# Block ends of the input projection set apart, its pools given back early, and 24 gate projections in front of the scan

## The chip, the core and the metric

One core of one Trainium2 chip runs the kernel. The metric is the device time of one execution in microseconds (us). PE is the matmul engine (TensorE), DVE VectorE, ACT ScalarE, POOL GpSimd, SP the queue that issues every DMA of this kernel.

## What is computed

One layer of a hybrid diffusion block, D = 1024, 2048 latent tokens behind 256 context tokens (2304 in all), float32. The first half matters here:

```python
h  = modulate(rmsnorm(x, norm1_g), shift1, scale1)      # and hc for the context
q, k, v, rw, gl = jnp.split(h @ w_in, IN_SPLITS, axis=-1)   # 512 | 128 | 128 | 1696 | 2048 columns
ya = latent_window_attention(q, k, v, kc, vc, sink)     # banded, |i-j| <= 128, plus all context keys
# rw: centred short conv, then decay, rate, key, value for RWKV-7
r_l, v_l, hg_l, kk_l, dirs_l = rwkv_prepare(short_conv(rw, conv_w), ...)
# one scan per direction; each latent scan starts from the context's final state
yr = rwkv_output(y_lat[0] + y_lat[1], ...)
ga, gr = sigmoid(gl) halves;  x = x + gate1 * ((ga * (ya @ Wa) + gr * (yr @ Wr)) @ Wo)
x = x + gate2 * sq_relu_mlp(modulate(rmsnorm(x, norm2_g), shift2, scale2), w_mlp_up, w_mlp_down)
```

The `gl` columns are the merge gates: 2048 columns for the 2048 latent tokens.

## The kernel before

Every large matmul runs in float32r with operands split in a high and a low part, three passes per k-tile (`gemm`, L210: lines 213, 214 and 215; k runs over 8 tiles, so one unit, 128 output columns for one token block, is 24 matmuls). ACT makes the high part of a weight (`w_hi`, L206), POOL the low part (`w_lo`, L207), from a 512 KB load (`w_raw`).

**First stage, the in-projection.** The 2304 tokens go in three passes of two token blocks each:

```python
THIRDS = (((0, 256), (256, 512)), ((1280, 384), (768, 512)), ((1664, 384), (2048, 256)))
```

(first token, number of tokens). `norm_block` (L170) loads a block's rows, scales them by the root mean square, transposes them on PE (`tr`, L184), modulates (`hf`, DVE) and splits into `hh` (ACT) and `hl` (POOL, L191). `hh`/`hl` have one buffer for the first block of a pass (tag a) and one for the second (tag b), so a block of the next pass can be written only when the block that held its buffer has had its last projection. `project` (L236) loads one 128-column group of weights after the other and uses each for all blocks that it is given. There are 36 groups: 0 to 13 the RWKV input `u`, 14 k, 15 v, 16 to 19 q, 20 to 35 the gates. Pass 0 and 1 run groups 0 to 19 for both blocks, then the gates for the one block that lies at or beyond latent token 1024, in pass 1 (1280, 384) alone; pass 2 runs its gates for both blocks at its very end. The gates of latent tokens 0 to 1023 aren't made here: `norm_block` writes those tokens' normed rows to DRAM (`h_d`).

`prepare` (L326) makes the scan's inputs for one window of 256 tokens: short conv, decay, keys, on DVE, ACT and POOL, with small matmuls (`ss`, `snt`, `vt`, `nb`, `zz`, `bon`) between; its results go to DRAM (`ka_d`, `rho_d`, `bk_d`, `v_d`). Windows 0 and 1 follow pass 0's projections, 2 to 5 pass 1's, 8, 7, 6 stand between pass 2's groups 0 to 19 and its gates in the program.

**Second stage, the scan.** 36 steps of 64 tokens, in both directions, in nine windows of four steps. For a window, `gram` (L504) loads `kg` and `bkg` and multiplies them into `ga`; `inverse` (L517) turns them into a triangular inverse, a chain of 31 pairs of DVE operations on `tn` and `itmp` (L531, L533) behind four transposes into `au` (L525). `before` prepares a step, `chain` (L617) advances the state: `ch` matmuls, L621 the first. Beside the steps, `beside(w)` places attention (one block of 128 queries per call), pieces of a modulation vector, and the gates of latent tokens 0 to 1023 as `gate` (L845): 4 blocks of 256 tokens times 16 column groups = 64, six per call in calls 0 to 10, each with its own weight load and split (`gw_hi`, `gw_lo`) and 24 matmuls of 256 columns.

**What sets the order.** The program is written in the sequence above, and a scheduler then fixes the instructions of each engine in one static order, from the waits that it derives; an engine never passes an instruction that waits. A pool gives memory that a later pool reuses, and the later pool's tiles wait for the release of what lay there. Before, all pools of the first stage are closed together (L480), after the last preparation and the last projection in the program; the scan's tiles (`rp`) lie where `hh` and `hl` were.

## Time and profile before

| | us |
|---|---|
| median of 3 runs (4350.85 to 4358.86) | 4355.5 |
| the profiled execution | 4356.59 |
| its span, first to last instruction | 4354.8 |
| PE busy | 3996.6 |
| first stage | 0 to 995 |
| from its last projection to the first `ch` matmul | 995 to 1129 |
| scan with attention and gates | 1129 to 2510 |
| output projections and MLP | 2510 to 4354 |

A view by stretches gives, for each stretch, the width and each engine's busy time in it, then the granted TensorE clock (1.00 is 2.4 GHz, 0.50 is 1.2 GHz). A matmul's listed duration is longer than the distance to the next one's start, since matmuls are pipelined; the cost of one in a row of them is the distance of the starts. A view of waits gives, for an engine, what its instructions waited for, total, times and the longest. In a timeline the brackets hold the idle time before the instruction and what ended it.

### The profile page before, as it was taken

To read this page: it belongs to the slowest core of one execution; us is meant where nothing else is said; L and a number is where in the kernel's file an instruction comes from. 1 tells how busy PE (TensorE), PEld (TensorE's weight loads), DVE (VectorE), ACT (ScalarE), POOL (GpSimd) and SP (SyncE) were. 2 spreads that over 40 slices of the span, in tenths; PEclk is the share of its full clock that TensorE was granted. 3 is DMA by queue.
4 is the path that set the end of the run, shared out by engine and by line. 5 is a ranking of instruction groups with operands and counts; after the bars stand their busy time and mean duration, and the time that the engine had idled before them with its cause. 6 is when DMAs were issued, how large, how long until landed. Compare 5 with 4: busy or idle time off the path is not lost.

```text
span 4354.8 us, 68914 instructions
## 1 busy us (share of the span) xinstructions
PE 3996.6 (92%) x27020; PEld 3152.5 (72%) x27020; DVE 2330.7 (54%) x3905; ACT 1339.7 (31%) x2390; POOL 1580.1 (36%) x1276
## 2 busy tenths in 40 slices
PE   7989969894999999999999969998999999999999
PEld 5868858783766666666666646777888888888887
DVE  2264286687567747657756446444443436443434
ACT  3353444553333233332222223332222123212121
POOL 3353554552332222322111146523433234433332
PEclk8979979895999989999999968999999999999999
DMA  6555556666644544555443245452211113221111
GB/s 216 142 187 158 160 158 189 175 198 185 160 137 139 149 137 119 162 141 154 146 135 97 84 142 185 157 178 75 82 54 58 39 54 121 73 63 49 48 49 49
DMA packets 633081, 544.70 MB, mean 125 GB/s; under 512 B 120500, under 2 KB 560532, under 8 KB 631732
## 3 DMA queue, kind: packets, MB, share of 16 engines
q1 hardware_dynamic: 632756, 540.29, 41.8%
q8 instruction: 213, 3.49, 0.3%
q14 instruction: 112, 0.92, 0.1%
HBM read 399.96 MB, written 140.18 MB: 124 GB/s over the span
## 4 chain that ended last, share of the span: by engine, by line
PE 58%; DVE 10%; DMA 4%; issue 2%; POOL 2%; ACT 1%; SPq 1%; POOLq 0%; DVEq 0%; ACTq 0%
PE fd L1186 5%; PE fd L1187 5%; PE fd L1188 5%; PE fu L213 5%; PE fu L214 5%; PE fu L215 5%; PE ops L791 3%; PE gb L610 2%; DVE tn L533 2%; DVE itmp L531 1%; DVE st L542 1%; PE sT L781 1%; PE mm L1101 1%; PE mm L1103 1%; PE mm L1102 1%
## 5 line engine op out<-in xcount | busy, mean ns | idle before, releaser
L213 PE MATMUL acc<-hh,w_hi 128*128 128x384 f32 (+6 forms) x1304 | 457.8, 353 | 27.7 <-DVE st L225 9.8
L214 PE MATMUL acc<-hl,w_hi 128*128 128x384 f32 (+6 forms) x1304 | 458.4, 352 | 11.2 <-POOL hl L191 7.4
L215 PE MATMUL acc<-hh,w_lo 128*128 128x384 f32 (+6 forms) x1304 | 453.3, 349 | 10.9 <-POOL w_lo L207 9.7
L1192 DVE TENSOR_TENSOR acc<-fd,acc 128x512 f32<-128x512 f32 x480 | 322.3, 686 | 246.6 <-PE fd L1188 244.0
L1176 DVE TENSOR_TENSOR g_l<-rl,g_h 128x512 fp32r<-128x512 f32 x128 | 163.0, 1275 | 486.1 <-POOL rl L1175 486.1
L213 PE MATMUL fu<-h2h,up_h 128*128 128x512 f32 x1024 | 403.3, 394 | 5.8 <-ACT rl L1173 5.8
L214 PE MATMUL fu<-h2l,up_h 128*128 128x512 f32 x1024 | 402.6, 393 | 0.0
L1186 PE MATMUL fd<-dn_h,g_h 128*128 128x512 f32 x1024 | 399.4, 390 | 3.0 <-DVE acc L1190 3.0
L215 PE MATMUL fu<-h2h,up_l 128*128 128x512 f32 x1024 | 402.0, 393 | 0.0
L1187 PE MATMUL fd<-dn_l,g_h 128*128 128x512 f32 x1024 | 399.4, 390 | 0.0
L1188 PE MATMUL fd<-dn_h,g_l 128*128 128x512 f32 x1024 | 397.8, 390 | 0.0
L1175 POOL TENSOR_TENSOR rl<-rl 128x512 f32<-128x512 f32 x128 | 146.6, 1146 | 473.6 <-ACT g_h L1174 473.5
L832 POOL TENSOR_TENSOR gw_lo<-gw_raw,gw_hi 128x1024 fp32r<-128x1024 f32 x64 | 152.3, 2381 | 441.5 <-ACT gw_hi L831 359.8
L207 POOL TENSOR_TENSOR w_lo<-w_raw,w_hi 128x1024 fp32r<-128x1024 f32 (+1 forms) x92 | 224.2, 2439 | 226.0 <-ACT w_hi L206 208.0
L213 PEld LDWEIGHTS acc<-hh,w_hi 128*128 128x128 f32 (+2 forms) x1304 | 257.3, 198 | 51.3 <-DVE st L225 7.8
L214 PEld LDWEIGHTS acc<-hl,w_hi 128*128 128x128 f32 (+2 forms) x1304 | 258.1, 198 | 34.2 <-POOL hl L191 12.3
L215 PEld LDWEIGHTS acc<-hh,w_lo 128*128 128x128 f32 (+2 forms) x1304 | 256.4, 197 | 32.7 <-POOL w_lo L207 11.6
L1173 ACT ACTIVATE rl<-fu 128x512 f32<-128x512 f32 x128 | 76.3, 598 | 661.0 <-PE fu L215 652.0
L1130 POOL TENSOR_TENSOR dn_l<-raw,dn_h 128x1024 fp32r<-128x1024 f32 x64 | 155.6, 2450 | 275.0 <-ACT dn_h L1129 275.0
L793 POOL TENSOR_TENSOR ts<-ts,pT 128x512 f32<-128x512 f32 x124 | 159.1, 1287 | 263.9 <-ACT pT L788 261.9
L213 PEld LDWEIGHTS fu<-h2h,up_h 128*128 128x128 f32 x1024 | 193.0, 188 | 49.3 <-ACT rl L1173 6.1
L1186 PEld LDWEIGHTS fd<-dn_h,g_h 128*128 128x128 f32 x1024 | 192.6, 188 | 44.2 <-DVE acc L1190 3.4
(301 smaller groups left out, 9154.7 us busy)
## 6 DMA issues: line engine op xcount, KB each, us to landing
w_raw<-in_w_in SPq DMA_DIRECT2D x74, 512.0 KB
gw_raw<-in_w_in SPq DMA_DIRECT2D x64, 512.0 KB
raw<-in_w_mlp_up SPq DMA_DIRECT2D x64, 512.0 KB
raw<-in_w_mlp_down SPq DMA_DIRECT2D x64, 512.0 KB
bk_d<-bk SPq DMA_DIRECT2D x36, 512.0 KB
bkg<-bk_d SPq DMA_DIRECT2D x72, 256.0 KB
w<-v_d SPq DMA_DIRECT2D x144, 128.0 KB
ada_w<-in_w_ada SPq DMA_DIRECT2D x32, 512.0 KB
```

The source lines that it names most:

```text
L207: pool.tensor_tensor(out=lo[:, :, :m], in0=raw[:, :, :m], in1=hi[:, :, :m].bitcast(F32), op=ALU.subtract)
L213: pe.matmul(ps[:m, :n], wh[:, k, :m], hh[:, k, :], start=(k == 0), stop=False)
L214: pe.matmul(ps[:m, :n], wh[:, k, :m], hl[:, k, :], start=False, stop=False)
L215: pe.matmul(ps[:m, :n], wl[:, k, :m], hh[:, k, :], start=False, stop=(k == KC - 1))
L793: pool.tensor_tensor(out=ts[:, g], in0=ts[:, g], in1=pT[g], op=ALU.add)
L832: pool.tensor_tensor(out=lo, in0=raw, in1=hi.bitcast(F32), op=ALU.subtract)
L1130: eng.tensor_tensor(out=lo, in0=raw, in1=hi.bitcast(F32), op=ALU.subtract)
L1176: dve.tensor_tensor(out=glo[:, j], in0=rl, in1=gh[:, j].bitcast(F32), op=ALU.subtract)
L1186: pe.matmul(ps, lh, dn[j][0][:, cs], start=(j == 0), stop=False)
L1187: pe.matmul(ps, lh, dn[j][1][:, cs], start=False, stop=False)
L1188: pe.matmul(ps, ll, dn[j][0][:, cs], start=False, stop=(j == FG - 1))
L1192: dve.tensor_tensor(out=acc[:, cs], in0=ps, in1=acc[:, cs], op=ALU.add)
```

## The change

Three edits.

The in-projection. From pass 1 on, groups 0 to 3 run for one block, then for the other, then groups 4 to 13 for both; at the end of pass 0 and 1, groups 14 to 19 (and the gates, where the block has them) run for one block, whose successor is then normed, and after that for the other, whose successor is normed next. `FIRST` says which ends first: in pass 0 the block of tag a, in pass 1 that of tag b. Weights of a group that serves the blocks one after the other are loaded and split twice: 112 loads in all where there were 92. The context block has no q, but `project` loads and splits a group's weights ahead of the test that skips it, so four loads of pass 0 serve no matmul.

The pools. `prep` and `prp` keep a stack of their own; all others of the first stage are in `pg1`, closed before it. The second stage's `attn`, `gates` and three PSUM pools open between the two closings; `rp`, `chp` and `auxp` (scan) open behind `p1.close()` and now lie where the preparation's tiles were.

The gates. 24 of the 64 gate projections stand in the program ahead of the scan's loop; the other 40 go four per call in calls 0 to 9.

```diff
     prep = p1.enter_context(tc.tile_pool(name="prep", bufs=1, side="right"))
-    wpool = p1.enter_context(tc.tile_pool(name="w1", bufs=2, side="right"))
-    xpool = p1.enter_context(tc.tile_pool(name="xin", bufs=4, side="right"))
+    prp = p1.enter_context(tc.tile_pool(name="prp", bufs=3, space=PSUM, side="right"))
+    pg1 = ExitStack()
+    wpool = pg1.enter_context(tc.tile_pool(name="w1", bufs=2, side="right"))
+    xpool = pg1.enter_context(tc.tile_pool(name="xin", bufs=4, side="right"))
...
-    hs = norms(THIRDS[0])
+    FIRST = (0, 1)
+    HEAD = 4
+    hs = [norm(0, 0), norm(0, 1)]
     for i, wins in enumerate(ready):
-        project(THIRDS[i], hs, groups[:20])
-        late = [(b, h) for b, h in zip(THIRDS[i], hs) if b[0] >= CTX + GL8R]
-        if i + 1 < len(THIRDS):
-            project(*zip(*late), groups[20:]) if late else None
-        if i + 1 < len(THIRDS):
-            hs = norms(THIRDS[i + 1])
+        blks = THIRDS[i]
+        if i == 0:
+            project(blks, hs, groups[:14])
+        else:
+            f = FIRST[i - 1]
+            project(blks[f:f + 1], hs[f:f + 1], groups[:HEAD])
+            project(blks[1 - f:2 - f], hs[1 - f:2 - f], groups[:HEAD])
+            project(blks, hs, groups[HEAD:14])
+        if i + 1 < len(THIRDS):
+            nxt = [None, None]
+            for b in (FIRST[i], 1 - FIRST[i]):
+                late = groups[20:] if blks[b][0] >= CTX + GL8R else []
+                project(blks[b:b + 1], hs[b:b + 1], groups[14:20] + late)
+                nxt[b] = norm(i + 1, b)
+            hs = nxt
+        else:
+            project(blks, hs, groups[14:20])
...
-    p1.close()
+    pg1.close()
...
     p2 = ExitStack()
-    rp = p2.enter_context(tc.tile_pool(name="rp", bufs=2, reuse_waits="tile"))
+    pg = ExitStack()
     ap_ = p2.enter_context(tc.tile_pool(name="attn", bufs=1, reuse_waits="tile"))
-    chp = p2.enter_context(tc.tile_pool(name="chp", bufs=1, space=PSUM, reuse_waits="tile"))
-    auxp = p2.enter_context(tc.tile_pool(name="auxp", bufs=2, space=PSUM, reuse_waits="tile"))
+    gap = pg.enter_context(tc.tile_pool(name="gates", bufs=1, reuse_waits="tile"))
...
+    p1.close()
+    rp = p2.enter_context(tc.tile_pool(name="rp", bufs=2, reuse_waits="tile", side="right"))
+    chp = p2.enter_context(tc.tile_pool(name="chp", bufs=1, space=PSUM, reuse_waits="tile", side="right"))
+    auxp = p2.enter_context(tc.tile_pool(name="auxp", bufs=2, space=PSUM, reuse_waits="tile", side="right"))
...
+    EARLY = 24
+    for t0, g in gate_work[:EARLY]:
+        if g == 0:
+            hs = load_h(t0)
+        gate(t0, g, *hs)
...
-        for t0, g in gate_work[6 * w:6 * w + 6]:
+        for t0, g in gate_work[EARLY + 4 * w:EARLY + 4 * w + 4]:
```

How the instructions stand at three places, the kernel before first and the changed one second each time.

**Place 1, POOL at the end of pass 0**, behind the `w_lo` of k for the context block. `w_lo_1313` is v before; in the changed kernel 1313, 1320, 1327 and 1334 are the context's unused q weights and 1431 is k for block (256, 512). `hl_1280` is the low part of pass 1's first block, `sw` and `st` belong to the rotary embedding of q, `sn` to the preparation.

```order
L207 TENSOR_TENSOR w_lo_1313<-w_raw_1315,w_hi_1314 128x1024
L207 TENSOR_TENSOR w_lo_1383<-w_raw_1385,w_hi_1384 128x1024
L224 TENSOR_TENSOR sw_1304<-sw_1304,cs_1302 128x512
L226 TENSOR_TENSOR st_1301<-st_1301,sw_1304 128x512
L207 TENSOR_TENSOR w_lo_1427<-w_raw_1429,w_hi_1428 128x1024
L207 TENSOR_TENSOR w_lo_1471<-w_raw_1473,w_hi_1472 128x1024
L224 TENSOR_TENSOR sw_1418<-sw_1418,cs_1416 128x512
L191 TENSOR_TENSOR hl_1280_1560<-hf_1589,hh_1280_1559 128x384
L226 TENSOR_TENSOR st_1415<-st_1415,sw_1418 128x512
L207 TENSOR_TENSOR w_lo_1515<-w_raw_1517,w_hi_1516 128x1024
L224 TENSOR_TENSOR sw_1462<-sw_1462,cs_1460 128x512
L191 TENSOR_TENSOR hl_1280_1560<-hf_1597,hh_1280_1559 128x384
```

```order
L208 TENSOR_TENSOR w_lo_1313<-w_raw_1315,w_hi_1314 128x1024
L366 TENSOR_TENSOR sn_1888<-sn_1888,expo_78 128x16
L208 TENSOR_TENSOR w_lo_1320<-w_raw_1322,w_hi_1321 128x1024
L192 TENSOR_TENSOR hl_1280_1342<-hf_1371,hh_1280_1341 128x384
L192 TENSOR_TENSOR hl_1280_1342<-hf_1379,hh_1280_1341 128x384
L208 TENSOR_TENSOR w_lo_1327<-w_raw_1329,w_hi_1328 128x1024
L192 TENSOR_TENSOR hl_1280_1342<-hf_1387,hh_1280_1341 128x384
L192 TENSOR_TENSOR hl_1280_1342<-hf_1395,hh_1280_1341 128x384
L208 TENSOR_TENSOR w_lo_1334<-w_raw_1336,w_hi_1335 128x1024
L192 TENSOR_TENSOR hl_1280_1342<-hf_1403,hh_1280_1341 128x384
L192 TENSOR_TENSOR hl_1280_1342<-hf_1411,hh_1280_1341 128x384
L208 TENSOR_TENSOR w_lo_1431<-w_raw_1433,w_hi_1432 128x1024
```

Before, splits whose groups serve (256, 512) follow one another; now four unused splits, the six `hl` and the `sn` stand between the context's v and the next split that a matmul needs.

**Place 2, PE at the end of pass 1**, where the last projection of (1280, 384) ends. `acc_4369` is its last unit before; `acc_6207@2048` the third unit of pass 2's head groups in the changed kernel.

```order
L215 MATMUL acc_4369<-hh_1280_1559,w_lo_4363 128x384
L360 MATMUL ss_ps_4954<-c1_1763,ksq_4971 128x2 x2
L213 MATMUL acc_6035<-hh_1664_4397,w_hi_6030 128x384
L360 MATMUL ss_ps_4954<-c1_1763,ksq_4981 128x2 x2
L360 MATMUL ss_ps_4954<-c1_1763,ksq_4991 128x2 x2
L214 MATMUL acc_6035<-hl_1664_4398,w_hi_6030 128x384
L215 MATMUL acc_6035<-hh_1664_4397,w_lo_6029 128x384
L213 MATMUL acc_6035<-hh_1664_4397,w_hi_6030 128x384
L184 MATMUL tr_4455<-ident_76,x_4399 128x128
L184 MATMUL tr_4455<-ident_76,x_4407 128x128
L184 MATMUL tr_4455<-ident_76,x_4415 128x128
L214 MATMUL acc_6035<-hl_1664_4398,w_hi_6030 128x384
```

```order
L214 MATMUL acc_6207<-hh_2048_3700,w_hi_6202 128x256
L215 MATMUL acc_6207<-hl_2048_3701,w_hi_6202 128x256
L454 MATMUL bon_ps_5391<-ks_5282,c1_1803 128x256
L185 MATMUL tr_4633<-ident_76,x_4577 128x128
L185 MATMUL tr_4633<-ident_76,x_4585 128x128
L185 MATMUL tr_4633<-ident_76,x_4593 128x128
L185 MATMUL tr_4641<-ident_76,x_4577 128x128
L185 MATMUL tr_4641<-ident_76,x_4585 128x128
L185 MATMUL tr_4641<-ident_76,x_4593 128x128
L216 MATMUL acc_6207<-hh_2048_3700,w_lo_6201 128x256
L214 MATMUL acc_6207<-hh_2048_3700,w_hi_6202 128x256
L215 MATMUL acc_6207<-hl_2048_3701,w_hi_6202 128x256
```

Before, the transposes of (1664, 384) stand inside the first unit of pass 2, which needs them; now they stand inside units of block (2048, 256), normed earlier, and units of (1664, 384) come four units later.

**Place 3, DVE between the last preparation and the scan.** `au`, `itmp` and `tn` are the inverse of window 0; `mm`, `pack`, `atmp`, `qB`, `rr` belong to attention block 0; `ka`, `rho`, `bk`, `ks` to the last preparation.

```order
L437 TENSOR_TENSOR ks_8363<-ta_8377,x3_8162 128x256
L525 STREAM_TRANSPOSE au_9643<-ga_9530 32x1024 x4
L425 SCALAR_TENSOR_TENSOR ka_8369<-kk_8361,ep_8382 128x4x64
L427 TENSOR_TENSOR rho_8370<-x3_8162,ep_8382 128x4x64
L437 TENSOR_TENSOR ks_8368<-ta_8399,x3_8172 128x256
L425 SCALAR_TENSOR_TENSOR ka_8369<-kk_8366,ep_8404 128x4x64
L427 TENSOR_TENSOR rho_8370<-x3_8172,ep_8404 128x4x64
L430 TENSOR_TENSOR bk_8371<-bk_8371,cum_8380 128x4x64
L438 TENSOR_TENSOR bk_8371<-ks_8363,cum_8380 128x4x64
L428 SCALAR_TENSOR_TENSOR bk_8421<-ta_8427,kk_8361 128x4x64
L430 TENSOR_TENSOR bk_8371<-bk_8371,cum_8402 128x4x64
L531 TENSOR_TENSOR itmp_9650<-tn_9644,au_9643 128x31
```

```order
L774 TENSOR_REDUCE mm_11371<-sc1_11436 128x1
L774 TENSOR_REDUCE mm_11371<-sc0_11435 128x1
L775 TENSOR_TENSOR mm_11371<-mm_11371 128x8
L776 TENSOR_TENSOR pack_11369<-mm_11371,nsink_9632 128x8
L777 TENSOR_TENSOR mm_11371<-sinkb_9633,pack_11369 128x8
L782 TENSOR_TENSOR atmp_11450<-mt_11448,cc_83 72x512
L789 TENSOR_TENSOR qB0_9653<-atmp_11450,qB0_9653 8x512 x2
L787 TENSOR_TENSOR rr0_9655<-atmp_11450,rr0_9655 8x512
L543 STREAM_TRANSPOSE au_9774<-ga_9661 32x1024 x4
L549 TENSOR_TENSOR itmp_9781<-tn_9775,au_9774 128x31
L551 TENSOR_TENSOR tn_9775<-tn_9775,itmp_9781 128x31
```

Before, the inverse starts in the middle of the last preparation; now it stands behind all of it (its last row is ten rows ahead of this piece) and behind attention block 0's row maxima.

## Rows read from the trace of the kernel before

**Rows 1.** The page, busy time of each engine, its share and instructions.

```profile
PE 3996.6 (92%) x27020; PEld 3152.5 (72%) x27020; DVE 2330.7 (54%) x3905; ACT 1339.7 (31%) x2390; POOL 1580.1 (36%) x1276
```

**Rows 2.** By stretches: width, PE, PEld, DVE, ACT, POOL busy, clock, DMA share, GB/s.

```profile
195.00:330.00 135.00, 118.34 (x515) 94.08 (x514) 81.66 (x144) 70.59 (x140) 79.85 (x83) 0.82 0.59 185
...
520.00:680.00 160.00, 116.58 (x585) 104.47 (x584) 125.77 (x233) 71.83 (x161) 82.03 (x90) 0.82 0.59 171
...
995.00:1129.00 134.00, 66.53 (x640) 52.96 (x641) 93.84 (x188) 45.57 (x94) 43.29 (x52) 0.63 0.57 165
1129.00:2510.00 1381.00, 1298.02 (x14059) 911.76 (x14055) 883.62 (x1680) 402.90 (x723) 349.95 (x241) 0.97 0.48 136
2510.00:4354.00 1844.00, 1772.68 (x7712) 1437.16 (x7712) 816.99 (x1038) 443.63 (x650) 714.00 (x486) 0.97 0.28 87
```

**Rows 3.** PE's waits in 520 to 680: total us, times, longest.

```profile
PE tr L184 <- DVE x L178: 11.0, 1, 11.0
PE acc L213 <- ACT w_hi L206: 4.8, 2, 4.6
PE acc L215 <- POOL w_lo L207: 4.7, 3, 2.5
PE acc L214 <- POOL hl L191: 2.8, 4, 1.4
PE acc L213 <- ACT hh L190: 2.7, 2, 1.5
PE tr L184 <- DVE hf L186: 2.4, 1, 2.4
```

**Rows 4.** PE's waits in 320 to 530, the one for weights.

```profile
PE acc L215 <- POOL w_lo L207: 2.3, 1, 2.3
```

**Rows 5.** Weight and block splits: count, duration in ns (least/median/most), first and last start.

```profile
L206 ACT ACTIVATE w_hi<-w_raw x86: 616/1057/1077, 104.1 to 975.8; 128x1024 fp32r<-128x1024 f32 x80, 128x512 fp32r<-128x512 f32 x3, 128x768 fp32r<-128x768 f32 x3
L207 POOL TENSOR_TENSOR w_lo<-w_raw,w_hi x86: 1283/2404/4042, 105.5 to 977.5; 128x1024 fp32r<-128x1024 f32 x80, 128x512 fp32r<-128x512 f32 x3, 128x768 fp32r<-128x768 f32 x3
...
L191 POOL TENSOR_TENSOR hl<-hf,hh x32: 729/1009/3647, 205.4 to 646.0; 128x384 fp32r<-128x384 f32 x16, 128x512 fp32r<-128x512 f32 x8, 128x256 fp32r<-128x256 f32 x8
```

**Rows 6.** PE's timeline near 986: start, duration; 256 and 384 columns.

```profile
986.04 0.28 PE L214 MATMUL acc<-hl,w_hi 128*128 128x256 f32 x1
986.16 0.28 PE L215 MATMUL acc<-hh,w_lo 128*128 128x256 f32 x1
...
986.63 0.34 PE L213 MATMUL acc<-hh,w_hi 128*128 128x384 f32 x1
986.81 0.34 PE L214 MATMUL acc<-hl,w_hi 128*128 128x384 f32 x1
```

**Rows 7.** PE's waits in 995 to 1129, two of them.

```profile
PE sc L746 <- DVE qA L732: 19.8, 1, 19.8
...
PE g L514 <- DMA bkg<-bk_d: 12.9, 4, 8.5
```

**Rows 8.** Timelines of DVE and PE: five marks from the last preparation to the scan.

```profile
995.06 0.17 DVE L364 TENSOR_SCALAR sn<-ss_ps 128x16 f32<-128x16 f32 x1 [5.89 <-PE ss_ps L360]
...
1036.70 7.62 DVE L525 STREAM_TRANSPOSE au<-ga 32x1024 f32<-32x1024 f32 x4
...
1056.45 0.42 DVE L454 TENSOR_TENSOR bon<-bon_ps,x 128x256 f32<-128x256 f32 x1
...
1099.42 6.08 DVE L542 STREAM_TRANSPOSE st<-tn 32x1024 f32<-32x1024 f32 x3
...
1128.79 0.27 PE L621 MATMUL ch<-w,kr 128*64 128x64 f32 x1
```

**Rows 9.** Timelines of DVE and POOL near 1079: the inverse beside a weight split.

```profile
1079.02 0.42 DVE L531 TENSOR_TENSOR itmp<-tn,au 128x247 f32<-128x247 f32 x1
...
1079.69 2.53 DVE L533 TENSOR_TENSOR tn<-tn,itmp 128x247 f32<-128x247 f32 x1
...
1079.59 4.84 POOL L832 TENSOR_TENSOR gw_lo<-gw_raw,gw_hi 128x1024 fp32r<-128x1024 f32 x2 [0.88 <-DMA ada_w<-in_w_ada]
```

More of the change, by code (lines that the diff above doesn't have):

```diff
@@ L151, in tile_hybrid_block @@
                                  op0=ALU.add, op1=ALU.mult)
[L153 to L157 removed]
+    hpool = pg1.enter_context(tc.tile_pool(name="hT", bufs=1))
+    epool = pg1.enter_context(tc.tile_pool(name="ev", bufs=2))
+    acc = pg1.enter_context(tc.tile_pool(name="acc", bufs=3, space=PSUM))
+    trp = pg1.enter_context(tc.tile_pool(name="trp", bufs=2, space=PSUM))
     def rstd_of(pl, x, tag, ss=None, sqtag=None, sqbufs=1):
@@ L458, in tile_hybrid_block, with norm @@
     ready = ((0, 1), (2, 3, 4, 5), (8, 7, 6))
-    def norms(blocks):
-        return [norm_block(t0, n, "a" if i == 0 else "b") for i, (t0, n) in enumerate(blocks)]
-    hs = norms(THIRDS[0])
-    for i, wins in enumerate(ready):
-        project(THIRDS[i], hs, groups[:20])
-        late = [(b, h) for b, h in zip(THIRDS[i], hs) if b[0] >= CTX + GL8R]
-        if i + 1 < len(THIRDS):
-            project(*zip(*late), groups[20:]) if late else None
-        if i + 1 < len(THIRDS):
-            hs = norms(THIRDS[i + 1])
+    def norm(i, b):
+        return norm_block(*THIRDS[i][b], "ab"[b])
+    FIRST = (0, 1)
+    HEAD = 4
+    hs = [norm(0, 0), norm(0, 1)]
+    for i, wins in enumerate(ready):
+        blks = THIRDS[i]
[6 more added lines that the diff above has]
+            project(blks, hs, groups[HEAD:14])
+        if i + 1 < len(THIRDS):
+            nxt = [None, None]
[6 more added lines that the diff above has]
+            project(blks, hs, groups[14:20])
         if i == 0:
@@ L900, in tile_hybrid_block @@
     mods = (x for m in range(4) for x in ada2(m))
-    pg = ExitStack()
-    gap = pg.enter_context(tc.tile_pool(name="gates", bufs=1, reuse_waits="tile"))
+    EARLY = 24
[3 more added lines that the diff above has]
+        gate(t0, g, *hs)
     seen = done = 0
```

5 lines of the change are left out of this document (removed).

## The prediction, made before the changed kernel was run

> **What bounds the kernel now.** I read the page's engine shares first: PE is busy 92% of the span, the next engine 54% [rows 1]. So PE is the engine to ask about, and the question is where it stands idle or runs at half clock. The view by stretches answers that [rows 2]. The stages behind 2510 and the scan are full: in the scan PE is busy 1298 of 1381 us at clock 0.97, so its matmuls set its length, and work taken out of it shortens it. Three stretches are not full. In 195 to 330 (pass 0 hands over to pass 1) PE is idle 135 - 118.3 = 16.7 us at clock 0.82. In 520 to 680 (pass 1 to pass 2) it is idle 43.4 us, also at 0.82. In 995 to 1129, between the last projection and the first `ch`, it is idle 67.5 us, and what it does runs at a mean clock of 0.63. The view of waits names causes: in 520 to 680, 11.0 + 2.8 + 2.7 + 2.4 = 18.9 us for the next pass's blocks (`x`, `hl`, `hh`, `hf`) and 9.5 us for weights [rows 3]; in 995 to 1129 for DVE and for DMAs, on work that stands in line behind it [rows 7]. The change aims at all three. The order of instructions is the same as before up to the last groups of pass 0 and again from the output projections on, so nothing of 0 to 195 or behind the scan is counted.
>
> **What a unit costs.** In a row of matmuls starts lie 0.12 us apart at 256 columns and 0.18 at 384 [rows 6]; a unit of 24 is 2.9 and 4.3 us. A weight group costs ACT 1.06 and POOL 2.40 us (medians), one `hl` step POOL 1.01 [rows 5].
>
> **First block end (+5).** Removed: the wait of pass 1's first units for a norm that runs beside nothing of its own. Added: the context block alone takes six loads, for two units. On POOL four unused splits and the one for the next matmul stand behind v, with six `hl`: 5 x 2.40 + 6 x 1.01 = 18 us. PE has v's unit (2.9 us) and transposes for about 3 more: a hole of 12 where 16.7 were idle, so +5. Ends: -12 (the hole comes on top, the old idle stays) and +38 (all 16.7 idle and the clock's 118.3 x 0.18 = 21 come back). I take the lower part because the hole stands in POOL's order and no other unit can pass it on PE.
>
> **Second block end (+20).** Block (768, 512) now ends first and its successor (2048, 256) is normed under 22 units of (1280, 384), 94 us of PE work: hidden. The norm of (1664, 384) lies under four units of (2048, 256), 11.5 us, while POOL needs 4 x 2.40 + 8 x 1.01 = 17.7 for both: a hole of 6. Of the 18.9 us of waits for blocks, with their share of the clock's loss (116.6 x 0.18 = 21, of which 18.9/43.4 is 9), 28 us go; the hole and its clock give 8 back. Ends 0 and +43 (all idle). The waits for the preparation's own DVE work stay; they were never those of the blocks.
>
> **More loads (-10).** 112 loads instead of 92: 20 x 1.06 on ACT, 20 x 2.40 = 48 us on POOL, 10 MB on SP's queue. These engines aren't full, so most is hidden beside matmuls. What shows is the waiting of a group that serves one block: the 16 gate groups of pass 1 were the only such ones, and PE waited 2.3 + 4.8 + 4.7 = 11.8 us for weights around them [rows 3, 4], 0.74 us each. Now there are 56 (6 + 6 in pass 0; 26 + 10 in pass 1; 8 in pass 2), 40 more: 0 to 30 us. I take 10, since 16 of the 40 serve 512 tokens, more matmul time over each load than the 384 of those gate groups, and four serve none.
>
> **The gap and the scan (+10).** By PE's order, 18 gates now stand ahead of the first `ch`, where five and a half stood: 12.5 x 2.9 = 36 us, with the rest of attention block 0 and the scores of block 1 (about 12 us, estimated from their matmul counts) some 48 us of PE work leave the scan. There PE is busy 94%; I count 42 us, less than 48, because chain and inverse now and then set the pace there.
>
> Against that stands the start of the scan. Before, `rp` lay where `hh` was, and grams ran beside the last preparation: from `sn` at 995.1 to the transposes `au` at 1036.7, the preparation's last DVE row at 1056.5, the inverse over at 1099.4, the first `ch` at 1128.8 [rows 8]: 134 us behind the last projection. Now `rp` waits for the preparation's tiles, and DVE and SP have grams and inverse behind all of it. Counted from the last projection's end: `sn` stands nearly three units ahead of it (22 of 24 matmuls at 256 columns, a unit at 384, one at 256), -10. The preparation took 61.4 us with `au` (7.6) in it and PE's gram waits; with those out and up to seven gate splits in, 58. Grams: before, 41.6 us from `sn`, of which PE waited 12.9 for their loads [rows 7] and the preparation had its share; now eight times 384 KB, with what else SP issues there about 5 MB, 30 us at the stretch's 165 GB/s [rows 2], which holds idle time too; I take 22. From `au` to its end 62.7 us, less the preparation's rows in it (8), plus the collisions with POOL: before, DVE's 0.42 us operation took 2.53 beside a weight split [rows 9], and eleven more splits stand there, up to 26 us, of which I take 12: 66. The rest, 29.4, as before. Sum 165: the scan starts 31 us later relative to the last projection. 42 - 31 = 11, as +10. Ends: +42 (no later start) and -16 (58 later). The clock in the gap rises from 0.63 with the gates, which shortens the PE steps of this path; I let that cover the waits of the path's matmuls behind gates in PE's one order.
>
> The Trainium skill, page "SBUF — State Buffer", section "SBUF: two separate sides", says that a DVE operation with two SBUF inputs and a GpSimd operation that reads SBUF share a port pair, that one of them holds it for its whole instruction, and that the other stands still meanwhile. The trace agrees for the one case above (2.53 against 0.42 us). By this rule each of the 20 added splits would hold DVE up by its whole 2.40 us, the third rival below with 4368; my sum has 4330.
>
> **Sum.** 5 + 20 - 10 + 10 = 25 us. The profiled execution took 4356.6 us with a span of 4354.8, 1.1 us over the median of 4355.5, so I subtract from the median: 4330. With the ends near (first 0 to 10, second 10 to 28, loads 0 to 18, gap 0 to 20) the forecast's own range is 4305 to 4346.
>
> **Rivals.**
> 1. *All holes close.* The blocks' norms hide wholly (+12 and +30), loads cost nothing, and the scan starts only 10 us later (+32): 74 us, 4281. For it: DVE is busy only 94 of 134 us in the gap and POOL 43 [rows 2], so both have room. Against: the path there is one chain, not a matter of room.
> 2. *A later start eats the gates.* All eleven splits fall on the inverse, and the preparation stretches behind the gates' POOL work: 50 us later, gap -8, total 7: 4348. For it: the collision in the trace, and the order on DVE. Against: the gates' own loads come at intervals, so splits needn't stand back to back.
> 3. *POOL holds DVE up in the passes.* Slower: each added split delays a preparation operation on DVE, and PE, one order for projections and preparation, waits behind `bon` and `zz`. Price 20 x 2.40 = 48 instead of 10: 25 - 38 = -13, 4368. It decides, against the other +35, from 35/20 = 1.75 us of lost time per added split. For it: DVE is busy 126 of 160 us in 520 to 680 [rows 2], and the collision had its full length [rows 9]. Against: in 320 to 530, where most of the lone groups of before ran, PE waited only 2.3 us for weights [rows 4].
>
> **Chances.** Forecast 0.49, rival 1 0.16, rival 2 0.18, rival 3 0.17. A measurement of this kernel tells about 0.2% (8.7 us) from no change: faster is under 4346.8. Faster: nearly all of the forecast (0.47), rival 1, and 0.07 of rival 2: 0.70. Same: 0.15 (rival 2 most). Slower: 0.15, nearly all from rival 3. The range goes from just under rival 1 to rival 3, 4275 to 4368; outside lie the better half of rival 1 and the worse half of rival 3, 0.15 to 0.17.
>
> **What would show it.** First end: a PE hole near 215 with POOL on `w_lo` and no unit running (right: 8 to 15 us). Second end: no wait of `tr` for `x` as long as 11 us between 520 and 680; idle there under 30. Loads: PE's waits for `w_hi` and `w_lo` by 10 us more over the first stage. Gap: first `ch` between 150 and 185 us behind the last projection, 18 gates ahead of it, PE's clock above 0.8; the scan, from the first `ch` on, about 1339 us. The prediction is wrong if the last projection doesn't end by 975 to 985, where 25 - 10 = 15 puts it, or if the first `ch` starts where it did relative to it (then rival 1) or over 185 us behind (rival 2).

## The result: slower by 0.9%

The changed kernel took 4396.3 us (median of 4 runs, 4393.1 to 4406.2) beside 4355.3 for the kernel before (4 runs on the same chip): ratio 1.009, 95% interval 1.0074 to 1.0106. The forecast was 4330 with a range of 4275 to 4368 and 0.15 on slower. It was wrong in sign, and the time lies outside the range.

The page of the changed kernel, which answers [rows 1]: PE's busy time is up by 12.5 us, its share down by a point, POOL has 20 instructions and 59 us more.

```profile
PE 4009.1 (91%) x27020; PEld 3174.4 (72%) x27020; DVE 2381.5 (54%) x3905; ACT 1361.0 (31%) x2410; POOL 1639.5 (37%) x1296
```

The view by stretches of the changed kernel, columns as in [rows 2]: the two block ends, then the stages, cut at the last projection, the first `ch`, the last `ch` and the first matmul behind the scan.

```profile
195.00:330.00 135.00, 104.93 (x441) 84.89 (x441) 84.19 (x122) 70.72 (x127) 92.10 (x86) 0.82 0.69 207
520.00:680.00 160.00, 121.51 (x638) 110.21 (x639) 121.66 (x202) 74.54 (x156) 97.48 (x83) 0.87 0.66 190
...
0.00:1021.00 1021.00, 861.39 (x4628) 753.85 (x4629) 573.56 (x1003) 467.84 (x947) 524.36 (x519) 0.90 0.62 182
1021.00:1209.00 188.00, 128.40 (x1020) 103.98 (x1018) 130.13 (x209) 67.43 (x127) 86.99 (x70) 0.77 0.63 175
1209.00:2551.00 1342.00, 1248.17 (x13637) 883.49 (x13635) 857.77 (x1652) 377.72 (x682) 307.69 (x215) 0.94 0.46 131
2551.00:2601.00 50.00, 35.30 (x167) 22.53 (x163) 18.38 (x31) 14.37 (x22) 32.85 (x30) 0.82 0.61 169
```

The same cuts in the kernel before:

```profile
994.00:1129.00 135.00, 67.53 (x649) 53.90 (x650) 93.84 (x188) 45.85 (x94) 43.29 (x52) 0.63 0.56 164
1129.00:2504.00 1375.00, 1298.02 (x14059) 911.76 (x14055) 880.35 (x1676) 402.90 (x723) 349.75 (x240) 0.97 0.48 136
2504.00:2568.00 64.00, 35.36 (x127) 27.26 (x128) 16.28 (x31) 7.23 (x11) 20.46 (x20) 0.53 0.45 128
```

Read each row as three parts: the width less PE's busy time is idle; busy time times one less the clock is lost to the clock (about 7 us uncertain in the scan, the clock has two digits); the rest is work at full clock.

| stretch | before | after | change | forecast |
|---|---|---|---|---|
| to the last projection | 994 | 1021 | +27 | -15 |
| gap, to the first `ch` | 134 | 188 | +54 | +31 |
| scan, to the last `ch` | 1375 | 1342 | -33 | -42 with the next |
| tail, to the first matmul behind it | 64 | 50 | -14 | |
| the rest | 1787 | 1790 | +3 | 0 |

The gap did not get fuller, it got longer: idle went from 67.5 to 59.6 us, work from 67.5 x 0.63 = 43 to 128.4 x 0.77 = 99, and it grew by as much as its work. In the scan 1298 x 0.97 = 1259 became 1248 x 0.94 = 1173: 86 us of work left, but the stage is only 33 shorter, since idle rose by 17 (77 to 94) and the clock's loss by 36 (39 to 75). Gap, scan and tail together are 7 us longer, the first stage 27; the two profiled executions are 36.6 us apart (4354.8 and 4391.4), the medians 41.

### The profile page after: what moved, and what is told of

Its sections match the earlier page's. It is cut to its first block, busy times and chain, and to the rows that moved or that the text cites. A ratio compares the mean times of both kernels' runs of the same rounds, so it can differ in the third digit from the quotient of the medians.

```text
span 4391.4 us, 68997 instructions
## 1 busy us (share of the span) xinstructions
PE 4009.1 (91%) x27020; PEld 3174.4 (72%) x27020; DVE 2381.5 (54%) x3905; ACT 1361.0 (31%) x2410; POOL 1639.5 (37%) x1296
## 4 chain that ended last, share of the span: by engine, by line
PE 59%; DVE 9%; DMA 5%; issue 2%; POOL 2%; SPq 1%; ACT 1%; POOLq 0%; DVEq 0%; ACTq 0%
PE fd L1207 5%; PE fd L1208 5%; PE fd L1209 5%; PE fu L214 5%; PE fu L215 5%; PE fu L216 5%; PE ops L809 3%; PE gb L628 3%; PE sc L764 1%; DVE st L560 1%; DVE itmp L549 1%; PE sT L799 1%; PE mm L1124 1%; PE mm L1122 1%; PE mm L1123 1%
## 5 line engine op out<-in xcount | busy, mean ns | idle before, releaser
L208 POOL TENSOR_TENSOR w_lo<-w_raw,w_hi 128x1024 fp32r<-128x1024 f32 (+1 forms) x112 | 271.9, 2429 | 237.3 <-ACT w_hi L207 225.3
L214 PEld LDWEIGHTS acc<-hh,w_hi 128*128 128x128 f32 (+2 forms) x1304 | 260.9, 200 | 76.7 <-ACT w_hi L207 23.7
```

The source lines that it names most:

```text
L208: pool.tensor_tensor(out=lo[:, :, :m], in0=raw[:, :, :m], in1=hi[:, :, :m].bitcast(F32), op=ALU.subtract)
L214: pe.matmul(ps[:m, :n], wh[:, k, :m], hh[:, k, :], start=(k == 0), stop=False)
```

## Experiments

Ratios are to the kernel before, timed in turn on the same chip; there its median was 4361 to 4365. "Joint" and "apart" speak of a block end; the heads are groups 0 to 3 run for each block by itself, and a lone group is one whose weights serve one block. The numbers by stage come from one profiled execution of each kernel. Kernels with the same passes differ there: the six with those of before end their last projection between 986 and 996, mean 992, so 5 us in one pair show little.

### The two halves of the change

The order of the passes alone, on the old pools with six gates per call, and its complement:

```diff
 # e1_order_only: the kernel before, with the changed loop over the passes
 # e2_gap_only: the changed kernel, with
+    hs = norms(THIRDS[0])
+    for i, wins in enumerate(ready):
+        project(THIRDS[i], hs, groups[:20])   # ... as before
```

> The kernel before with the changed order of the in-projection's passes alone; its pools, their single close and six gates per call stay. Theory (two separate bills: the passes lose 27 us, the later start of the scan loses the rest): the last projection ends near 1021 instead of 994.5, the first ch follows it after 134 us as before, total 4355 + 27 = 4382. Rival (the passes lose only together with the split pools): last projection by 1000, total 4355 to 4360. Second rival (the new order also pushes the last preparation behind the last projection): the first ch 150 us or more behind it, total 4395 or more.

Measured: 1.0119 (1.0098 to 1.014); last projection at 1023.6, first `ch` 139 behind it, scan 1404.

> The changed kernel with the order of the passes of before: only the pools given back in two parts and the 24 gates ahead of the scan are left of the change. Theory (two separate bills): last projection at 994.5 as before, first ch 180 to 190 us behind it instead of 134, scan from there 1342 us instead of 1377, total 4396 - 27 = 4369, which is 14 slower than before. Rival (the gap's price comes from the preparation that the new order pushed back): first ch 150 to 165 us behind, total 4335 to 4350.

Measured: 1.0045 (1.0023 to 1.0067); last projection at 992.7, first `ch` 201 behind it, scan 1362. Both halves cost. The passes lose their 29 us by themselves, with a gap only 5 us longer behind them, and pools with early gates lose on their own too; none of the rivals holds. But the bills (52 and 20 us) don't add up to the changed kernel's 41: the scan of e1_order_only is 29 us longer than before too, which no theory had.

### The first block end

PE's timeline of the changed kernel between the context's last unit and the next, then POOL's, then SP's (its idle time isn't shown):

```profile
186.66 0.28 PE L216 MATMUL acc<-hh,w_lo 128*128 128x256 f32 x1
...
200.88 1.86 PE L185 MATMUL tr<-ident,x 128*128 128x128 f32 x6 [2.34 <-DVE hf L187]
213.59 0.80 PE L214 MATMUL acc<-hh,w_hi 128*128 128x512 f32 x1 [10.85 <-ACT w_hi L207]
```

```profile
192.58 2.36 POOL L208 TENSOR_TENSOR w_lo<-w_raw,w_hi 128x1024 fp32r<-128x1024 f32 x1
194.89 1.96 POOL L192 TENSOR_TENSOR hl<-hf,hh 128x384 fp32r<-128x384 f32 x2
196.80 2.36 POOL L208 TENSOR_TENSOR w_lo<-w_raw,w_hi 128x1024 fp32r<-128x1024 f32 x1
...
201.03 2.35 POOL L208 TENSOR_TENSOR w_lo<-w_raw,w_hi 128x1024 fp32r<-128x1024 f32 x1
203.33 1.95 POOL L192 TENSOR_TENSOR hl<-hf,hh 128x384 fp32r<-128x384 f32 x2
213.62 2.37 POOL L208 TENSOR_TENSOR w_lo<-w_raw,w_hi 128x1024 fp32r<-128x1024 f32 x1 [8.34 <-ACT w_hi L207]
```

```profile
194.97 1.18 SPq L203 DMA_DIRECT2D w_raw<-in_w_in  x2
...
199.19 2.86 SPq L206 DMA_DIRECT2D w_raw<-in_w_in  x1
202.35 6.06 SPq L129 DMA_DIRECT2D x<-in_x  x3
208.50 0.39 SPq L206 DMA_DIRECT2D w_raw<-in_w_in  x1
```

No projection runs from 186.9 to 213.6: 26.7 us, with transposes of the next block in it. POOL is done with the unused splits and `hl` by 205.3 and then waits 8.3 us itself, for a weight that SP could issue only at 199.2, behind the loads of the unused groups, and that ACT has at 212.5, while three x loads go over the same queue. Three kernels take this apart:

```diff
 # e3_no_unused (in project)
+            if kind == "q" and all(t0 < CTX for t0, n in blocks):
+                continue
 # e11_unused_no_lo: loaded and on ACT, not split
+        if unused:
+            return hi, lo
         pool.tensor_tensor(out=lo[:, :, :m], ...)
 # e4_first_joint: pass 0's end and pass 1's beginning as before
+            if i == 0:
+                project(blks, hs, groups[14:20])
+                nxt = [norm(1, 0), norm(1, 1)]
```

> The changed kernel without the four q weight groups that the context block loads and splits in pass 0 and never multiplies. Theory (PE's hole from 187 to 214 stands behind these four on SP and POOL, the two weight buffers pass through them one by one): the hole shrinks from 26.8 us by four POOL splits of 2.4 us and the hl steps between them to about 14, total 4396 - 12 = 4384. Rival (the hole ends with the x loads of the next block, which stand ahead of the weight on SP's queue): hole 22 or more, total 4392 to 4398.

Measured: 1.001 (0.9995 to 1.0025). The pause behind the context's last unit is gone, not 14 us long; but another of 12.9 opens at 228.4: no projection runs until 241.3, behind matmuls of the preparation and the norm (before, the longest pause there is 4.6). The last projection is at 1002.2, 18.9 earlier than in the changed kernel. The total gained more, 36 us; between the two profiles, 29.5 us apart, the scan is 12 shorter, the part behind the tail 6, the gap 9 longer.

> The changed kernel with the context's four unused q groups still loaded and turned into w_hi on ACT, but not split on POOL. Theory of the prediction (POOL's splits make PE's hole behind the context block): the hole between 187 and 214 falls from 26.8 us to 16 or less. Rival (SP's order of loads makes it: the weight that PE waits for is issued behind the unused loads and three x loads): the hole stays at 22 or more.

Measured in one execution: the pause is 11.3 us instead of 26.7, last projection at 1006.3. PE's and SP's timelines of this kernel:

```profile
198.62 0.80 PE L216 MATMUL acc<-hh,w_hi 128*128 128x512 f32 x1 [0.77 <-ACT w_hi L207]
```

```profile
192.62 0.37 SPq L206 DMA_DIRECT2D w_raw<-in_w_in  x1
```

Without the four splits SP issues that weight 6.6 us earlier and PE starts 15.0 earlier. POOL's splits made this pause, as forecast, but not by their own time alone (four of 2.4 us): behind them stands the next load, which takes 13.3 us from issue to ACT's start in the changed kernel and 4.9 here. What makes it slow is open; the load after it takes 14.5 here.

But a shorter pause is not a gain of as much. PE's waits for weights between 186 and 260, the changed kernel's two and then this one's:

```profile
PE acc L214 <- ACT w_hi L207: 10.8, 1, 10.8
PE acc L216 <- POOL w_lo L208: 4.2, 2, 3.0
```

```profile
PE acc L218 <- POOL w_lo L210: 8.0, 4, 3.5
PE acc L216 <- ACT w_hi L207: 3.3, 2, 2.6
```

They fall from 15.0 to 11.3: most of the wait moved to the next weights. So the price of an end is read well behind it, at equal work: at the time by which the kernel before has done some number of projection columns, how many us later does another kernel reach the same number? For the work that the kernel before has done by 330, and for all of it:

| | at 330 | last projection |
|---|---|---|
| changed kernel | +15.8 | +26.7 |
| e11_unused_no_lo | +12.2 | +11.9 |
| e3_no_unused | +5.9 | +7.8 |
| e4_first_joint | -0.5 | -0.1 |

At the first end the four unused groups cost 10 us, their splits alone 3.6, little more than scatter (kernels with the first end as before lie between -1.6 and +4.0 at 330). The other 9 and 11 by which e3_no_unused and e11_unused_no_lo end their passes earlier arise in pass 2. There the changed kernel (as e1_order_only) waits for the rotary embedding `st` of q, whose `cs` loads are late. A row of DVE there, and PE's waits for `st` in 700 to 985, the changed kernel first, then e11_unused_no_lo:

```profile
875.57 0.56 DVE L226 TENSOR_TENSOR st<-acc,cs 128x384 f32<-128x384 f32 x1 [9.56 <-DMA cs<-in_rope]
```

```profile
PE acc L214 <- DVE st L226: 17.4, 3, 9.0
```

```profile
PE acc L216 <- DVE st L228: 5.9, 3, 3.4
```

Why the loads are late there in these two kernels and not in the others isn't shown.

> The changed kernel with the first block end as before (groups 14 to 19 of pass 0 for both blocks, both norms behind them, no heads in pass 1); the second end, the heads of pass 2, the pools and the gates stay changed. Theory (the traces stand 15 us apart at equal projection work behind the first end, 27 at the end): 15 us come back, total 4381, last projection near 1006. Rival (the passes are short of weight splits as a whole, a hole closed at one place opens at the next): under 5 come back, total 4391 to 4397.

Measured: 1.003 (1.0018 to 1.0043); last projection at 994.3. All 27 us of the first stage came back, not 15: 16 at the first end, as expected, and the rest in pass 2.

### The heads and the second block end

```diff
 # e8_no_heads: e4_first_joint with
-    HEAD = 4
+    HEAD = 0
 # e12_first_split: e3_no_unused with the same (both ends apart, no unused loads, no heads)
 # e17_second_end: the kernel before, with the passes of e8_no_heads
```

> As the run with the first block end joint, but without the four groups that (2048, 256) and (1664, 384) each run alone at the head of pass 2: eight weight loads and splits fewer. Theory (lone groups cost PE a wait for their weights; w_hi waits in 470 to 700 are 19.3 us with them and 4.8 in the kernel before): the w_hi waits there fall to 12 or less, last projection 5 to 10 us earlier than 994. Rival (the heads hide the second norm, PE now waits for it): a wait of tr or of acc for hh and hl of 8 us or more, last projection 5 or more later.

Measured: 0.9954 (0.9934 to 0.9973), last projection at 989.0; PE's waits for `w_hi` in 470 to 700 fall from 19.3 to 8.6 us. Eight lone groups fewer are 5 us there, no more than kernels with the same passes scatter, and no new wait reaches 8.

> As the run without heads, but with the first block end apart too, without the four unused loads. Theory (what the first end apart saves at the norm, it pays in loads for one block): last projection 992 to 998 beside 989 in the run without heads, total 3 to 8 over it, ratio 0.996 to 0.998. Rival (the forecast's +5 was right but for the unused loads): last projection 985 or earlier, ratio 0.994 or less.

Measured: 0.9998 (0.9983 to 1.0013), last projection at 985.4. Beside e3_no_unused (1002.2) only the heads are gone, 16 lone groups in two passes: 17 us, about one each, with the scatter of 5 or so. For the last projection the rival comes nearer, for the total it doesn't: the passes end no later than with the first end joint, and the scan behind them took 28 us more (1340 against 1312).

> The kernel before with the second block end apart alone (block (768, 512) ends first, no groups at the head of a block alone, first end as before, old pools, six gates per call). Theory of the prediction for this end (+20 by itself, +28 without the hole on POOL): last projection 966 to 975 instead of 994, total 4330 to 4337. Rival (the 11 us wait for the norm goes, waits for weights and for the preparation stay): last projection 985 to 991. For the total then: 4348 if the scan is left as it is, and 4365 to 4400 if the scan, whose order the scheduler makes anew, gets 15 to 50 us of idle time and low clock more, as in the other runs on the old pools.

Measured: 0.9988 (0.9975 to 1.0002), last projection at 990.0, scan 1382 us with PE idle 76 at clock 0.97, like before. So the second end apart is not worth 20 us. That it is worth 4 is not shown by one pair: seven kernels with this end of pass 1 and no heads, the first end joint, end their last projection between 983 and 994, mean 989.3, the six with the passes of before at 992.3 in the mean, 3 us apart. Its stretches and, in 520 to 680, PE's waits (to be read beside [rows 3]):

```profile
520.00:680.00 160.00, 130.01 (x665) 118.84 (x666) 111.37 (x195) 70.85 (x154) 89.94 (x82) 0.85 0.60 173
```

```profile
PE bon_ps L453 <- DVE ks L450: 8.0, 2, 5.4
PE acc L213 <- ACT w_hi L206: 6.9, 3, 4.4
PE acc L213 <- ACT hh L190: 5.7, 3, 4.9
PE acc L214 <- POOL hl L191: 3.3, 3, 2.6
PE tr L184 <- DVE hf L186: 2.1, 1, 2.1
```

The 11.0 us wait of `tr` for `x` is gone. The waits for `hh`, `hl`, `hf` and `w_hi` are 18.0 us, where `x`, `hl`, `hh`, `hf` and `w_hi` were 11.0 + 2.8 + 2.7 + 2.4 + 4.8 = 23.7. One long wait became several short ones. In the changed kernel, with its heads, a wait of the same norm for `hf` stands in its place (2.4 before); two of PE's waits in 520 to 680:

```profile
PE tr L185 <- DVE hf L187: 10.6, 5, 5.7
PE tr L185 <- DVE x L179: 0.5, 1, 0.5
```

### The gap

```diff
 # e5_gates_old_pools: the kernel before, with
+    EARLY = 24   (24 gates ahead of the steps, 4 per call, as in the change)
 # e6_pools_only: e2_gap_only with EARLY = 0 and 6 per call
 # e7_split_rp: e2_gap_only with a pool of its own for grams and inverse
+    rq = p2.enter_context(tc.tile_pool(name="rq", bufs=2, reuse_waits="tile"))
     gap = pg.enter_context(...)          # left, with auxp, gtp, chp
...
     p1.close()
     rp = p2.enter_context(... side="right"))   # rest of rp, attn, oup, atp
```

> The passes as before, the pools given back in two parts, six gates per call as before, none written ahead. Theory (rp's place on the preparation's memory makes the gap longer, and the order fills it with gates by itself): first ch 195 to 205 us behind the last projection, as in the run with the 24 gates (201), and the total within 8 us of that run's, 20 us over before. Rival (the 24 gates make the gap longer): first ch 150 to 170 behind, total within 5 of before.

Measured: 1.0012 (0.9992 to 1.0031); first `ch` 197 us behind the last projection, without a gate written ahead. The order puts 16 gates ahead of it by itself. The longer gap comes from the new division of the pools, not from the place of the gates in the program. The total does not follow the expectation: it is 0.3% under e2_gap_only, from the scan.

> As the run with passes of before, new pools and 24 gates, but the tiles of grams and inverse lie where the projections' tiles lay, beside the gates' (a pool of their own), and the attention's tiles wait for the preparation instead. 14 gates stand ahead of the first ch. Theory (the waiting of grams and inverse for the preparation's tiles costs 35 to 45 of the 67 us by which the start of the scan is later): first ch 150 to 165 us behind the last projection, from there 1400 to the start of the MLP, total 4325 to 4340. Rival (DVE beside the gates' splits on POOL is what makes it late): first ch 180 or more behind, total 4365 or more.

Measured: 0.9977 (0.9958 to 0.9996); first `ch` 142 behind the last projection, 14 gates ahead of it. Two rows of DVE's timeline and the gap's stretch:

```profile
1043.48 1.89 DVE L530 STREAM_TRANSPOSE au<-ga 32x1024 f32<-32x1024 f32 x1
...
1070.69 0.42 DVE L455 TENSOR_TENSOR bon<-bon_ps,x 128x256 f32<-128x256 f32 x1
```

```profile
990.00:1132.00 142.00, 90.06 (x799) 81.15 (x798) 101.57 (x165) 51.58 (x102) 62.84 (x57) 0.75 0.68 192
```

`au` starts 27 us ahead of the preparation's last row, as before and unlike the changed kernel, and the gates now fill idle time: the gap is 8 us longer than before with 23 us more busy time in it. The first `kg` load is issued at 988.2 here and at 1062.3 in e2_gap_only, behind the last `bon` (1057.9). So the wait of grams and inverse for the preparation's memory cost most of the 67 us: this division gives 59 back (201 to 142), but it also moves attention's tiles, some PSUM pools and eight gates out of the gap, which were not tried by themselves. The rival, splits beside DVE, wanted 180 or more and fails. The total is 10 us under before where 15 to 30 were expected.

> The kernel before with the 24 gates written ahead of the scan and four per call, its pools and passes as they were. In its order six gates stand ahead of the first ch, where five and a half stood. Theory (the pools, not the place of the gates in the program, set the order): no change, 4350 to 4360 beside 4355. Rival (24 gates written ahead take DVE's and POOL's time from the inverse): first ch 10 us or more later, total 4365 or more.

Measured: 1.0097 (1.0062 to 1.0131); first `ch` 132 behind the last projection, six gates ahead, scan 1425. Neither theory: the first `ch` isn't later, yet the total is 42 us over before.

### The scan

The scan and its tail were what upset the totals, so six kernels went there: the joined one (passes of e8_no_heads, pools of e7_split_rp), and the number of gates per call and ahead.

```diff
 # e9_joined: EARLY = 24, 4 per call      # e10_spread: 40 gates over 12 calls
 # e13_joined_six: EARLY = 0, 6 per call  # e16_joined_early_six: EARLY = 24, 6 per call
 # e14_no_heads_six: e8_no_heads, EARLY = 0, 6 per call
 # e15_old_pools_six: e5_gates_old_pools, EARLY = 24, 6 per call
```

> The passes of the run without heads (first block end joint, second end apart) together with the pool for grams and inverse of its own. Theory (the two gains lie in different stages and add up): ratio to before 0.9954 + 0.9977 - 1.0045 = 0.9886, some 50 us under before; last projection near 989, first ch 140 to 150 us behind it. Rival (fewer gates ahead of the first ch, 14 for 20, and DVE's work on the preparation beside the inverse take it back): ratio 0.993 to 0.997.

Measured: 0.9952 (0.9933 to 0.9971). First `ch` 138 behind the last projection (983.4), close to the expected 140; the total is the rival's.

> As the joined kernel, with the 40 gates behind the first 24 spread over twelve calls (three or four each) instead of ten calls of four. Theory (in the scan, PE's idle time and low clock sit where no gate is left: in the changed kernel 45.3 and 44.4 us in the 641 us behind the last gate, in the kernel before 23.9 and 15.4 in 524): the stretch behind the last gate gets 80 to 100 us shorter, idle and low clock in the whole scan fall by 8 to 20 us, ratio 0.002 to 0.005 under the joined kernel. Rival (the stretch with fewer gates per call idles more by as much): within 0.0015 of the joined kernel.

Measured: 1.0062 (1.0039 to 1.0084). Wrong in sign: with more gates late in the scan it got 41 us longer, by clock before all (0.95 to 0.93).

> As the joined kernel (passes without heads, a pool of its own for grams and inverse), but no gate written ahead of the scan and six per call, as in the kernel before. Theory (four gates per call instead of six is what makes the scan dearer by idle time and low clock; the joined kernel's total came to 0.9952 where the sum of its parts was 0.9886): ratio 0.985 to 0.991. Rival (the place of the gates doesn't matter, the scan's clock scatters from kernel to kernel): 0.9935 to 0.997 like the joined kernel.

Measured: 0.9976 (0.9962 to 0.9989), outside the theory, just above the rival.

> As the run without heads (new pools, 0.9954), but no gate written ahead and six per call. Theory (four per call is dearer than six by 0.33%, as between the runs with before's passes and new pools, 1.0045 and 1.0012): ratio 0.991 to 0.994. Rival (scatter of the scan): 0.9945 to 0.9975.

Measured: 0.994 (0.9917 to 0.9963), which doesn't tell the two apart.

> The kernel before with 24 gates written ahead, as in the run that came to 1.0097, but six per call behind them instead of four. Theory (the number per call is what costs): 0.998 to 1.003. Rival (writing 24 ahead costs, by leaving the back of the scan without gates): 1.006 or more.

Measured: 1.0095 (1.0071 to 1.0118), the rival's.

> As the joined kernel with its 24 gates ahead, but six per call behind them. Theory (number per call): 0.985 to 0.991, within 0.002 of the run with none ahead and six per call. Rival (gates ahead cost): 0.003 or more over that run.

Measured: 1.0037 (1.0018 to 1.0055), 0.006 over the run with none ahead, the rival's.

The number per call is not it: 24 ahead on the old pools cost 0.95% with six per call as with four, and on the joined kernel four come out 0.85% better than six (e9, e16). Gates ahead alone are not it either: none ahead is better by 0.6% in one pair (e13, e16), but e9 with 24 comes out no worse than e13 with none. The rows of the scans, of e17_second_end, e15_old_pools_six, e9_joined and e10_spread in this order:

```profile
1119.00:2501.00 1382.00, 1305.69 (x14081) 919.60 (x14081) 882.62 (x1676) 402.89 (x724) 352.79 (x242) 0.97 0.49 136
```

```profile
1128.00:2566.00 1438.00, 1334.18 (x14042) 940.33 (x14071) 884.78 (x1690) 405.95 (x730) 355.95 (x243) 0.94 0.47 130
```

```profile
1121.00:2490.00 1369.00, 1286.54 (x13876) 903.74 (x13875) 874.95 (x1689) 392.31 (x711) 330.55 (x231) 0.95 0.47 134
```

```profile
1128.00:2538.00 1410.00, 1317.58 (x13868) 927.72 (x13869) 894.85 (x1685) 389.38 (x704) 332.31 (x230) 0.93 0.46 130
```

The first two have the same matmuls to within 39, the last two to within 8. Work at full clock agrees too (1267 and 1254; 1222 and 1225). What differs is idle time (76 and 104; 82 and 92) and the clock (0.97 and 0.94; 0.95 and 0.93): 56 and 41 us of length. By their medians the kernels of the first pair are 47 us apart, 10 of which the profiles have ahead of the scan. Of the 19 profiled kernels the one before and e17_second_end have the least idle time in the scan (77 and 76 us) and the highest clock (0.97); the others have 82 to 113 and 0.92 to 0.96. On the old pools, with nearly the same work in the scan, e1_order_only, e5_gates_old_pools and e15_old_pools_six lose 52 to 74 us more by the two than before. The medians of e5_gates_old_pools (1.0097) and e15_old_pools_six (1.0095), whose first `ch` is no later than before, bear it out; that of e1_order_only (1.0119) holds the 29 us of its passes too. The order of the scan is another in all three, but in e17_second_end as well, which loses nothing: of the 1675 DVE operations of before's scan, at most 1188 stand in the same sequence there by the names of their tiles, 1120, 1107 and 1014 in the three. So kernels with nearly the same work in the scan differ by about 1% through idle time and clock, and that is shown; that the order is what does it is argued, and which part of it is open.

### What beats both

e14_no_heads_six (0.994), e9_joined (0.9952) and e8_no_heads (0.9954) are faster than both kernels; their intervals overlap. All three have the first end joint, the second apart and no heads; but so have e13_joined_six (0.9976), e16_joined_early_six (1.0037) and e10_spread (1.0062), so the passes don't decide it. e7_split_rp (0.9977), with the passes of before, is under the kernel before too.

## Why the prediction was wrong

**What bounds the kernel.** Right: PE with its idle time and clock. The work at full clock is the same within 3% in all profiles (first stage; gap, scan and tail together; the rest), and what a change moved is one of these two.

**First block end, +5.** The place and the engine were right (POOL on unused splits, no unit running), the size not: 26.7 us for 12. The step summed POOL's own 18 us and let the next weight be ready behind it. The load of that weight is issued only behind them, so its way through SP and ACT, with 8.3 us of POOL's own waiting, comes on top. At equal projection work the changed kernel is 15.8 us behind at 330. Of these the unused groups are 10, their splits alone 3.6, since the weights behind them are late as well; most of the rest are pass 1's heads (e12_first_split, without both, is 1.4 behind there). So the end apart by itself gave nothing where it was to give 5.

**Second block end, +20.** Failed, the largest gain of the first stage: 3 to 4 us alone (e17_second_end). The step took 28 us of wait and clock as a gain once the norm was hidden. The wait went, but waits for weights, for the next `hh` and `hl` and for the preparation stood just behind it. As what is late next the text named POOL's hole alone. The changed kernel has PE wait 10.6 us for `hf` there.

**More loads, -10.** Too small. PE's waits for `w_hi` and `w_lo` up to the last projection, before and changed:

```profile
PE acc L215 <- POOL w_lo L207: 9.7, 6, 2.5
PE acc L213 <- ACT w_hi L206: 6.1, 3, 4.6
```

```profile
PE acc L214 <- ACT w_hi L207: 20.8, 9, 10.8
PE acc L216 <- POOL w_lo L208: 19.2, 13, 3.5
```

That is 24 us more, where 10 were named. By the last projection the 16 heads cost 17 and the four unused groups 19, of which 10 at the first end. The price of 0.74 put 11.8 us of waits on 16 gate groups; a head is about 1.05, an unused group 2.5 at the first end. Without these 20 loads both ends apart gave 985 (e12_first_split) beside 986 to 996 in six kernels with the passes of before (mean 992): 7 us, about the scatter of such kernels, where the terms for the ends had 25.

**Gap, -31.** Came to -54. The four marks of the changed kernel on DVE, and the first `ch`, to be read beside [rows 8]:

```profile
1008.99 0.17 DVE L365 TENSOR_SCALAR sn<-ss_ps 128x16 f32<-128x16 f32 x1 [8.05 <-PE ss_ps L361]
...
1083.52 0.41 DVE L455 TENSOR_TENSOR bon<-bon_ps,x 128x256 f32<-128x256 f32 x1
...
1117.93 7.99 DVE L543 STREAM_TRANSPOSE au<-ga 32x1024 f32<-32x1024 f32 x4 [8.04 <-ACT ga L533]
...
1179.17 7.84 DVE L560 STREAM_TRANSPOSE st<-tn 32x1024 f32<-32x1024 f32 x4
...
1209.21 0.33 PE L639 MATMUL ch<-w,kr 128*64 128x64 f32 x2
```

`sn` stands 12 ahead of the last projection (forecast 10). The preparation took 75 us from there (58), the grams 34 (22), the inverse 61 (66), the rest 30 (29.4). Preparation and grams were mis-sized by 29. With the same passes and no gates beside it (e1_order_only) the preparation took 51, from 1011.46 to 1062.83; so 24 us come from what the order puts into it: six gate splits on POOL and attention's first operations on DVE. Two rows of DVE and POOL there:

```profile
1041.92 2.50 DVE L426 SCALAR_TENSOR_TENSOR ka<-kk,ep 128x256 f32<-128x256 f32 x1
```

```profile
1041.45 2.69 POOL L850 TENSOR_TENSOR gw_lo<-gw_raw,gw_hi 128x1024 fp32r<-128x1024 f32 x1
```

The same operation takes 0.42 elsewhere in this preparation. The Trainium skill, page "SBUF — State Buffer", section "SBUF: two separate sides", has one engine hold the shared port pair for its whole instruction; here the trace agrees, 2.50 beside a split of 2.69. The grams waited for SP: the first `kg` was issued at 1091.29, 7.4 us behind the last `bon`, after gate loads and stores in SP's one queue.

**Gates leaving the scan, +42.** Scan and tail together gave 47, so the size came out right, by two errors. Some 86 us of work left the scan, not 48 (by clocks of two digits, so 10 more or less; the gap's work rose by 56, the tail's by 10), and 53 of them came back as idle time and clock. I took 48 to 42 with PE's busy share of before at hand, which holds only if what stays is as dense as what leaves.

**The rivals.** The second (a later start eats the gates) came nearest for the gap: 54 later for its 50. The third (POOL holds DVE up in the passes) had the sign, by the wrong way: PE's waits for `bon` in the first stage were 33.5 us (34.4 before), and what grew were those for weights. No case joined a loss in the passes with a late start, though the bounds that stood in the text (-12, 0, -30, -16) add up to 4413.5. The range ended at the worst single rival; terms that fail together needed the sum. The forecast's own range was too narrow in the same way: its near ends add up to 4298 to 4364, not to 4305 to 4346.

**The marks named ahead.** Right: no `tr` for `x` of 11 us (0.5 in the changed kernel), 18 gates ahead, and nearly the scan (1342 to the last `ch`; the 1339 ran some 6 us past it, so 1333). Wrong: the waits for weights (24 more for 10), the hole (26.7 for 8 to 15), idle in 520 to 680 (38.5 for under 30), the clock in the gap (0.77 for over 0.8), the last projection (1021 for 975 to 985), the first `ch` (188 behind for 150 to 185).

## What to carry to other kernels

A wait that ends last hides those that end just before it: credit its removal only with the distance to the next one, read in the same stretch for every engine that feeds the waiting one. Work moved into a gap shortens the kernel only if the gap doesn't grow by as much, so ask first what sets the gap's length; here a division that put the scan's pool on memory freed late made it 67 us longer, and another division gave 59 back. A pause is no price: one got 15 us shorter and the kernel 3.6 us faster behind it, so read what a change is worth at equal work, well behind the place.

## What the runs showed of the hardware

The granted clock of one stage with the same matmuls was 0.97 in one kernel and 0.94 in another (scans of e17_second_end and e15_old_pools_six), with idle time of 76 and 104 us; together this is 56 us, 1.3% of the kernel's time. Executions of one and the same kernel move with it: e2_gap_only ran from 4356.6 us at a mean clock of 0.943 to 4403.6 at 0.935. These are 47 us between runs of one kernel, so single profiles of two kernels can differ by tens of us without a cause in the change, and totals here rest on medians of 4 to 12 runs, but for e11_unused_no_lo's one.
